# Value tiles ahead of the attention, and three more weight pairs in seven-product form

## The chip, the cores and the metric

The kernel runs on one core of one Trainium2 chip. The core has a matrix engine (TensorE, "PE" in the profile; its weight loads are "PEld"), a vector engine (VectorE, "DVE"), a scalar engine (ScalarE, "ACT"), GpSimd ("POOL") and SyncE ("SP"), which mostly issues transfers. All run beside each other, each in the order of its own queue, and wait for each other by semaphores. The metric is the time of one execution on the device in microseconds; lower is better. Matrix operands lie in the on-chip memory, matrix results in accumulator banks of 128 x 512 fp32, and inputs, outputs and the scratch tensors named `..._d` in DRAM.

## The reference

One layer of a hybrid backbone on two token groups that share the weights: 128 context tokens and 512 latent tokens (an 8 x 64 grid), 1024 channels. Cut to what matters:

```python
h = x * (1 + scale) + shift                       # modulation from c
z = h @ w_in                                      # 1024 -> 4*1024 + 4*1024 + 2*1024
hy, g_h, qkv, g_a, m = split(z)
y_h = (fft_conv(v_h * x1) + u * d) * x0           # Hyena branch, after a 3-tap convolution
q, k, v = qkv                                     # 16 heads of 64
y_a = softmax(q k^T / 8 + bias) v                 # latents: 8 x 16 window and 128 cached keys
p_h = (y_h * silu(g_h)) @ w_bh
p_a = (y_a * silu(g_a)) @ w_ba
out = (sigmoid(m_h) * p_h + sigmoid(m_a) * p_a) @ w_out
x_new = layer_norm(ALPHA * x + gate * out)
```

Returned are the new tokens of both groups and the context group's keys and values. Everything is fp32. The kernel splits an operand into a rounded high half and a low half and takes three passes for a product (high x high, high x low, low x high).

## The kernel before, in words

All 640 tokens are one matrix: `hH` and `hL`, the halves of `h`, hold 8 tiles of 128 channels by 640 tokens and stay on the chip. A weight tile `wall[i]` is 128 x 1024 and gives 128 output channels. A **standard projection** (`proj`, line 168, or line 182 with the low weights last) takes 8 channel tiles x 3 passes x 2 halves of 320 tokens. Its weights come through `wtile`: a load into `raw` (two buffers), a rounded copy `wh` (two buffers) by ScalarE, and a low half `wl` (three buffers), either by VectorE (`split`, lines 101 and 102) or, with `eng="dma"`, as a negated copy by ScalarE to which POOL issues a DMA that adds the raw tile (lines 147 to 149).

A **seven-product pair** (`pair_tile`, line 1146) computes two weight tiles at once. The 2 x 2 blocks (two tiles by two halves of the tokens, with four channel tiles on either side of the sum) are multiplied with seven products of 4 x 3 matmuls. It needs sums of weights (four on VectorE, line 1111, and seven high and low halves), sums of the results (lines 1155 and 1161), and **token sums** t1 to t4 of `hH` and `hL`, made once by `token_sums(r)` for r = 0 and 1 and kept as high and low halves. `prepare` readies a pair's weights; `follow` names the next pair, so that it is prepared while the present one runs.

A **value tile** (`values(m)`, lines 842 to 857) has the tokens as the stationary side and 256 output columns, for four heads: 2 weight tiles, 2 x (48 + 12) matmuls.

The stages: a prologue (modulation), 24 convolution projections with filters and long convolutions beside them, the **hand-over**, the attention, and three projections with the final norm. In the hand-over the main line of work is the last quarter's gated convolution projections, then queries 0, keys 0, values 0, gate 0, queries 1, values 1 and keys 1, with `token_sums(0)` next to the last two. The side line is the last long convolution and `attention_setup`, which gives up the convolution's memory and opens the pools of the attention (`sp`, `at`, `tp`). `weave(main, side, n_main, n_side)` takes n_side steps of the side for n_main steps of the main line. Here a planner orders each engine's instructions, from modelled times; `keep_in_program_order` ties one instruction behind the one traced before it on its engine.

The attention is written for eight pairs of heads (`attend(j)`: scores, softmax, transposes, products with the values one head pair later), each woven with a main line from `mains(j)`: for 0 gate 1, queries 2, keys 2 and `token_sums(1)`; for the others seven-product pairs, with values 2 in 3 and values 3 in 5. There TensorE follows the order of the program (`manual_schedule`); the other engines are planned. Values of head pairs 2m and 2m + 1 come from value tile m, which has a slot of its own (`slot`).

Of the kernel before, what the change touches and what calls it, by code (L numbers as in the profile page):

```python
# [18 lines left out]
NK = 8  # L19
# [26 lines left out]
def tile_hyena_natten_step(ctx: ExitStack, tc: tile.TileContext, a, o):  # L46
# [3 lines left out]
    def f(ap):  # L50
        return ap.bitcast(F32)
# [13 lines left out]
        if pinned[0]:  # L65
            tc.keep_in_program_order(ins)

    def weave(main, side, n_main, n_side):
        done, taken = 0, 0
        for _ in main:  # L70
            done += 1
            while taken * n_main < done * n_side:
                if next(side, StopIteration) is StopIteration:
                    break
                taken += 1
        for _ in side:
            pass
# [34 lines left out]
    def load_pack(i):  # L112
        pack = const.tile([P, sum(n for _, n in PACKS[i])], F32, tag=f"pack{i}", name=f"pack{i}")
        load_to(pack[:], a[f"pack{i}"])
        c0 = 0
        for name, n in PACKS[i]:
            out[name] = pack[:, c0 : c0 + n]
            c0 += n

    load_pack(0)  # L120
    cc, sel = out["cc"], out["sel"]
# [614 lines left out]
    def chain(*gens):  # L736
        for g in gens:
            yield from g

    with tc.manual_schedule(engines={mybir.EngineType.PE, mybir.EngineType.DVE, mybir.EngineType.Activation}):  # L740
        prologue()
    tc.keep_in_program_order(last[0])
# [77 lines left out]

    def keys(j):
        cached_keys(j)
        for hf, p in enumerate((yield from proj(T_K + j, low_last=True))):
            k_half(j, hf, p[:, :HALF])
        yield

    def values(m):
        w = [wtile(T_V + 2 * m + i, width=256) for i in range(2)]
        ps = [acc(f"v{m}_{i}") for i in range(2)]
        v = slot(m, "v", f"v{m}")  # L830
        out[f"v{m}"] = v

        def passes(k):
            wh, wl = w[k // 4][0][k % 4], w[k // 4][1][k % 4]
            return ((hH, wh, k == 0, False), (hL, wh, False, False), (hH, wl, False, k == NK - 1))

        for half in range(2):
            ks = range(4 * half, 4 * half + 4)
            for k in ks:
                for x, wk, first, last in passes(k):  # L840
                    for t in range(4):
                        nc.tensor.matmul(  # L842
                            ps[t // 2][:, t % 2 * 256 : t % 2 * 256 + 256], x[:, k, P * t : P * t + P], wk,
                            start=first and t % 2 == 0, stop=last, skip_group_check=True,
                        )
                yield
            if half:
                for i in range(2):
                    nc.scalar.activation(v[:, 512 * i : 512 * i + 512], ps[i][:], AF.Copy)
# [6 lines left out]
        nc.scalar.activation(v[:, 1024:], pe[:, :256], AF.Copy)  # L856
        nc.sync.dma_start(o["new_v"][:, m * 256 : m * 256 + 256], v[:, :256])
        yield

    N_VALUES = 11  # L860

    def hand_over():
        yield from quarter_tail(3)
        hwa_stack.close()
        out["slots_l"] = left.enter_context(tc.tile_pool(name="slots_l", bufs=1))
        out["slots_q"] = left.enter_context(tc.tile_pool(name="slots_q", bufs=1))
        yield from chain(queries(0), keys(0), values(0), gate_a(0), queries(1))
        out["slots_r"] = left.enter_context(tc.tile_pool(name="slots_r", bufs=1))
        yield from alongside(chain(values(1), keys(1)), token_sums(0), 2)

    tail = ctx.enter_context(ExitStack())
    ac = ctx.enter_context(ExitStack())
    edges, biases = {}, {}

    def attention_setup():
# [3 lines left out]
        tp = left.enter_context(tc.tile_pool(name="tp", bufs=1))  # L879
        at = ac.enter_context(tc.tile_pool(name="at", bufs=1, side="right"))  # L880
        biases[0] = [bias_tile(h) for h in range(2)]
        for b, c in ((0, 0), (3, 320)):
            for h in range(2):
                edges[b, h] = at.tile([P, 384], F32, tag=f"edge{b}{h}", name=f"edge{b}{h}")
                nc.gpsimd.memset(edges[b, h][:, c : c + 64], 0.0)
        yield

    at = sp = tp = None

    def bias_tile(hd):  # L890
        tm = at.tile([P, 1024], F32, tag="tm", bufs=4, name=f"tm{hd}")
# [15 lines left out]
    def probs(j, b, s, tm):  # L907
        lo, hi = TWIN[b]
        res = []
        for h in range(2):  # L910
# [3 lines left out]
            ins = nc.vector.tensor_tensor_reduce(  # L914
                pv, s[h][:, : hi - lo], tm[h][:, lo:hi], -1.0, 3.0e38, ALU.add, ALU.min, accum_out=sm[:, 0:1]
            )
            if j < 2 and h == 0:
                tc.keep_in_program_order(ins)
            nc.scalar.activation(pv, pv, AF.Exp, scale=-1.0, bias=sm[:, 0:1], accum_out=sm[:, 1:2])
            nc.vector.reciprocal(sm[:, 2:3], sm[:, 1:2])  # L920
# [113 lines left out]
                yield  # L1034

    N_ATT = 4

    def gate_a(j):
        out[f"sg{j}"] = sg = at.tile([P, NT], F32, tag="sg", bufs=2, name=f"sg{j}") if j else row(yhp, "yh", "sg0")
        yield from gate_tile(T_GA + j, sg[:], low_last=True)  # L1040
        yield


    SUMS = ("t1", "t3", "t2", "t4")
    tok = {t: [[], []] for t in SUMS}

    def token_sums(r):
        def part(t, i, j):
            return f(t[:, 4 * i + 2 * r : 4 * i + 2 * r + 2, CS[j]])

        def step(dst, i, j, sign):
            for t in (hH, hL):
                nc.vector.tensor_tensor(dst, dst, part(t, i, j), op=ALU.add if sign > 0 else ALU.subtract)

        t1, t2 = (two(row(sp, "s", f"ts{r}{i}", bufs=2)[:]) for i in range(2))

        def keep(name, t):
            pools = [(yhp, "yh", NK + 1)] * 8 if r == 0 else [(tp, "tr", 4)] * 4 + [(sp, "tr", 3)] * 3 + [(at, "tr", 1)]
            for i in range(2):
                pool, tag, bufs = pools[2 * SUMS.index(name) + i]  # L1060
                tok[name][i].append(row(pool, tag, f"{name}_{r}{i}", F32R, bufs))
            split(two(tok[name][0][r][:]), two(tok[name][1][r][:]), t)

        tc.keep_in_program_order(nc.vector.tensor_tensor(t1, part(hH, 0, 1), part(hL, 0, 1), op=ALU.add))
        yield
        nc.vector.tensor_tensor(t2, t1, part(hH, 0, 0), op=ALU.subtract)
        nc.vector.tensor_tensor(t2, t2, part(hL, 0, 0), op=ALU.subtract)
        yield
        keep("t1", t2)
        yield  # L1070
        nc.vector.tensor_tensor(t1, part(hH, 1, 1), t1, op=ALU.subtract)
        nc.vector.tensor_tensor(t1, t1, part(hL, 1, 1), op=ALU.add)
        yield
        keep("t3", t1)
        yield
        step(t2, 1, 1, -1)
        yield
        keep("t2", t2)
        yield
        step(t2, 1, 0, 1)  # L1080
        yield
        keep("t4", t2)

    def operand(name):
        if name in tok:
# [111 lines left out]
    def qk_(j):  # L1197
        return T_Q + j, T_K + j
# [4 lines left out]
    def mix_(m):  # L1203
# [1 line left out]
        return t, t + 1  # L1205

    runs = (
        (mix_(0), qk_(3), mix_(1), qk_(4), ga_(2)), (mix_(2), qk_(5), mix_(3), ga_(4), qk_(6)),
        (mix_(4), qk_(7), mix_(5), ga_(6), mix_(6), mix_(7)),
    )  # L1210
    follow = {x: y for run in runs for x, y in zip(run, run[1:])}

    def alongside(main, side, every, first=0):
        for i, _ in enumerate(main):
            if i >= first and i % every == 0:
                next(side, None)
            yield
        for _ in side:
            pass
# [369 lines left out]
```

## Time and profile before

| | |
|---|---|
| median of 3 runs | 882.67 us (882.23 to 883.29) |
| the profiled execution | 883.84 us |
| its span, first to last instruction | 882.1 us |
| TensorE busy | 868.4 us, 6482 matmuls |
| VectorE busy | 638.4 us |
| ScalarE busy | 432.1 us |
| POOL busy | 129.2 us |
| DMA traffic | 129.21 MB |
| mean granted TensorE clock | 0.994 |

Busy time is the union of an engine's instructions. Matmuls overlap in the array, and their ends are modelled, so TensorE's pace is read from the starts of consecutive matmuls and not from their durations. The chain of work that ended last is followed back from the last instruction, at each step to what released it or to the instruction before it on its engine. In rows of groups of instructions stand the line, engine, operation, output <- inputs, shape and count, then the busy time, the mean of one in ns, and the engine's idle time before them with what ended it. Rows of one line or tile give the least, median and greatest duration in ns and the first and last start in us.

### The profile page before, as it was taken

What the parts mean: (1) busy time and instruction counts of PE and PEld (TensorE: products, weight loads), DVE (VectorE), ACT (ScalarE), POOL (GpSimd) and SP (SyncE); (2) the same over time, 40 slices, a digit from 0 to 9 for tenths busy, and PEclk for the clock granted to TensorE, in tenths of its full rate; (3) what the DMA queues carried; (4) which work ended last, traced back from release to release, by engine and by line L of the source; (5) the groups of instructions that cost most, each with busy time, mean ns of one, the idle gap of its engine ahead of it and who ended that gap; (6) DMA issues with size and microseconds to landing.
All of it is one profiled execution on the core that took longest, in us unless ns stands there. A gap on an engine that the chain in (4) does not pass through costs nothing.

```text
span 882.1 us, 16747 instructions
## 1 busy us (share of the span) xinstructions
PE 868.4 (98%) x6482; PEld 840.5 (95%) x6482; DVE 638.4 (72%) x1276; ACT 432.1 (49%) x926; POOL 129.2 (15%) x133
## 2 busy tenths in 40 slices
PE   8999999999999999999999999999999999999996
PEld 6899999999999999999999999999999999999885
DVE  4686687769559867699887667865788567676666
ACT  3485555645553433366665465655666632243200
POOL 0211010101000000035323222222222200000000
PEclk9999999999999999999999999999999999999999
DMA  9977666566566221262525143433262488446611
GB/s 308 379 193 164 133 134 129 135 142 144 122 145 135 75 93 55 73 216 84 165 75 174 55 151 101 141 106 122 81 191 72 134 307 282 159 151 200 214 59 61
DMA packets 55140, 129.21 MB, mean 146 GB/s; under 512 B 8304, under 2 KB 24436, under 8 KB 55061
## 3 DMA queue, kind: packets, MB, share of 16 engines
q1 hardware_dynamic: 45412, 107.76, 37.5%
q0 software_dynamic: 4032, 14.68, 10.3%
q10 hardware_dynamic: 5616, 5.70, 1.9%
q8 instruction: 51, 0.84, 0.4%
q14 instruction: 29, 0.23, 0.1%
HBM read 113.96 MB, written 14.16 MB: 145 GB/s over the span
## 4 chain that ended last, share of the span: by engine, by line
PE 92%; DVE 4%; DMA 2%; issue 1%; ACT 1%; SPq 0%; DVEq 0%; ACTq 0%
PE mm L168 38%; PE sp L1146 22%; PE out L1413 6%; PE v L842 5%; PE mm L182 3%; PE pt L939 2%; PE s L946 2%; PE s L899 2%; DMA ada<-wada 2%; PE ve L854 1%; PE adaT L251 1%; PE yb L157 1%; PE yb L158 1%; PE yb L156 1%; PE fl L455 1%
## 5 line engine op out<-in xcount | busy, mean ns | idle before, releaser
L1146 PE MATMUL sp<-t,wb 128*128 128x320 f32 x768 | 121.0, 311 | 0.8 <-DVE wb L102 0.8
L1146 PEld LDWEIGHTS sp<-t,wb 128*128 128x128 f32 x768 | 113.9, 188 | 1.6 <-DVE wb L102 1.1
L168 PE MATMUL mm<-hH,wh 128*128 128x320 f32 x480 | 113.8, 314 | 0.3 <-ACT hH L368 0.3
L168 PE MATMUL mm<-hL,wh 128*128 128x320 f32 x480 | 113.3, 312 | 0.0
L168 PE MATMUL mm<-hH,wl 128*128 128x320 f32 x480 | 113.1, 311 | 0.0
L1146 PE MATMUL sp<-hH,wb 128*128 128x320 f32 x384 | 93.2, 313 | 0.0
L168 PEld LDWEIGHTS mm<-hH,wh 128*128 128x128 f32 x480 | 80.6, 189 | 2.6 <-issue 1.4
L168 PEld LDWEIGHTS mm<-hL,wh 128*128 128x128 f32 x480 | 81.2, 189 | 0.9 <-DVE hL L376 0.4
L168 PEld LDWEIGHTS mm<-hH,wl 128*128 128x128 f32 x480 | 81.3, 189 | 0.5
L1146 PEld LDWEIGHTS sp<-hH,wb 128*128 128x128 f32 x384 | 66.0, 188 | 1.9 <-issue 1.9
L101 ACT ACTIVATE wh<-raw 128x1024 fp32r<-128x1024 f32 x31 | 32.9, 1060 | 63.9 <-PE mm L168 35.1
L921 POOL TENSOR_SCALAR p<-p,sm 128x384 f32<-128x384 f32 x32 | 44.9, 1413 | 110.1 <-DVE sm L920 96.2
L149 ACT ACTIVATE wh<-raw 128x1024 fp32r<-128x1024 f32 x28 | 29.8, 1063 | 62.0 <-PE mm L168 62.0
L1146 PE MATMUL sp<-hL,wb 128*128 128x320 f32 x192 | 59.3, 309 | 0.0
L148 POOL DMA_DIRECT2D wl<-wall x28 | 24.3, 869 | 220.9 <-ACT wl L147 160.2
L102 DVE TENSOR_TENSOR wb<-s,wb 128x512 fp32r<-128x512 f32 x64 | 44.6, 711 | 15.7 <-ACT wb L101 15.5
L101 ACT ACTIVATE wb<-s 128x512 fp32r<-128x512 f32 x64 | 39.2, 630 | 25.0 <-DVE s L1111 18.5
L101 ACT ACTIVATE wb<-raw 128x512 fp32r<-128x512 f32 x48 | 30.1, 628 | 35.1 <-PE sp L1146 20.6
L1413 PE MATMUL out<-woh,yhs 128*128 128x512 f32 (+1 forms) x176 | 45.5, 372 | 0.0
L921 POOL TENSOR_SCALAR edge<-edge,sm 128x320 f32<-128x320 f32 x32 | 44.3, 1396 | 2.2 <-DVE sm L920 2.1
L102 DVE TENSOR_TENSOR wl<-raw,wh 128x1024 fp32r<-128x1024 f32 x31 | 37.9, 1221 | 7.7 <-ACT wh L101 7.5
L168 PE MATMUL mm<-yhs,wh 128*128 128x320 f32 x224 | 42.0, 309 | 0.0
(365 smaller groups left out, 2162.2 us busy)
## 6 DMA issues: line engine op xcount, KB each, us to landing
raw<-wall SPq DMA_DIRECT2D x93, 512.0 KB, 3.6
wl<-wall POOLq DMA_DIRECT2D x28, 512.0 KB, 5.7
ada<-wada SPq DMA_DIRECT2D x16, 512.0 KB, 5.9
tm<-bias SPq DMA_DIRECT2D x16, 512.0 KB, 4.5
gate<-wgate SPq DMA_DIRECT2D x8, 512.0 KB, 4.1
wo<-wall SPq DMA_DIRECT2D x8, 512.0 KB, 4.2
xt<-xT SPq DMA_DIRECT2D x8, 320.0 KB, 7.4
dec<-decay SPq DMA_DIRECT2D x20, 128.0 KB, 3.1
```

Source lines behind the costliest of these rows:

```text
L101: hi = nc.scalar.activation(dst_h, src, AF.Copy)
L102: return hi, (eng or nc.vector).tensor_tensor(dst_l, src, f(dst_h), op=ALU.subtract)
L148: nc.gpsimd.dma_start(wl, a["wall"][i], accum_op=ALU.add)
L149: nc.scalar.activation(wh, raw[:], AF.Copy)
L168: nc.tensor.matmul(ps[hf][:, :HALF], wt[k], x[:, hf * HALF : (hf + 1) * HALF], start=(i == 0 and k == 0), stop=(i == lead[2] and k == NK - ...
L182: nc.tensor.matmul(p[:, :HALF], w[i // 2][k], (hH, hL)[i % 2][:, k, cs], start=n == 0, stop=n == len(steps) - 1, skip_group_check=True,)
L842: nc.tensor.matmul(ps[t // 2][:, t % 2 * 256 : t % 2 * 256 + 256], x[:, k, P * t : P * t + P], wk, start=first and t % 2 == 0, stop=last, ...
L899: nc.tensor.matmul(dst[h], x[rows(h), qs], y[rows(h), ks], start=i == 0, stop=i == 2, skip_group_check=True)
L921: nc.gpsimd.tensor_scalar_mul(pv, pv, sm[:, 2:3])
L939: nc.tensor.transpose(pt[:, i * P : i * P + P], x, ident)
L1146: nc.tensor.matmul(dst, wk, x(xi, k), start=j < 4 and k == 0 and i == 0, stop=k == 3 and i == 2, skip_group_check=True,)
L1413: ins = nc.tensor.matmul(dst, m[k][:, c0 : c0 + P], w[:, c : c + n], start=(first and k == 0), stop=(last and k == 5), skip_group_check=True,)
```

## The change

All four value tiles are computed in the hand-over, in the order 1, 2, 3, then queries 0, keys 0, values 0. Values 1, 2 and 3 are evicted into the slots that keys 0 takes later (`k`, `kl`), stored to a DRAM tensor `v_d`, and loaded into their own slots ahead of head pairs 0, 3 and 5 (`values_back`). The low halves of the weights for these tiles, for queries 0 and for keys 0 are made by the POOL-issued DMA (`eng="dma"`). Queries 1 and keys 1, queries 2 and keys 2, and gates 0 and 1 become seven-product pairs in the stages of head pairs 0 and 1; the following pairs with `mix` move accordingly, and all pairs form one chain of `follow`.

The token sums are made earlier: for r = 0 t1, t3, t2 and for r = 1 t1, t3 in `early_sums`, beside the value tiles, with scratch from the convolution's `u` buffers; t2, t4 for r = 1 and t4 for r = 0 in `late_sums`, after `attention_setup`, which waits for `early_sums` to have been written out. Where an operand of a later sum was given up, `again` adds its two halves. `weave` gets a parameter `late`, which holds the side back by one step of the main line in the stages of head pairs 2, 4 and 6. One reduction of head pair 0 is no longer tied to the program order.

```diff
-    def weave(main, side, n_main, n_side):
+    def weave(main, side, n_main, n_side, late=0):
...
-            while taken * n_main < done * n_side:
+            while taken * n_main < (done - late) * n_side:
...
+    def first_sums(r, out_):
+        t2, t1 = (scratch(True, f"ts{r}{i}") for i in range(2))
+        tc.keep_in_program_order(nc.vector.tensor_tensor(t1, part(hH, r, 0, 1), part(hL, r, 0, 1), op=ALU.add))
...
+    def early_sums():
+        t = []
+        yield from first_sums(0, t)
+        yield from second_sum(0, t[0])
+        yield from first_sums(1, t)
+        out["early_sums"] = True
+
+    def late_sums():
+        t = again("t1", 1)
+        yield from second_sum(1, t)
+        yield from third_sum(1, t)
+        yield from third_sum(0, again("t2", 0))
...
-        for hf, p in enumerate((yield from proj(T_Q + j, low_last=True))):
+        for hf, p in enumerate((yield from proj(T_Q + j, eng="dma", low_last=True))):
...
-        w = [wtile(T_V + 2 * m + i, width=256) for i in range(2)]
+        w = [wtile(T_V + 2 * m + i, "dma", width=256) for i in range(2)]
...
+        for i in range(3 if m else 0):
+            nc.sync.dma_start(v_d[m][:, 512 * i : min(512 * i + 512, 1280)], v[i])
...
+    def values_back(m):
+        out[f"v{m}"] = slot(m, "v", f"v{m}")
+        load_to(out[f"v{m}"][:], v_d[m])
...
-        yield from chain(queries(0), keys(0), values(0), gate_a(0), queries(1))
-        out["slots_r"] = left.enter_context(tc.tile_pool(name="slots_r", bufs=1))
-        yield from alongside(chain(values(1), keys(1)), token_sums(0), 2)
+        tp = left.enter_context(tc.tile_pool(name="tp", bufs=1))
+        yield from alongside(chain(values(1), values(2), values(3), queries(0), keys(0), values(0)), early_sums(), 1)
...
     def attention_setup():
-        nonlocal at, sp, tp
+        nonlocal at, sp
+        while "early_sums" not in out:
+            yield
         hy.close()
...
-            if j < 2 and h == 0:
+            if 0 < j < 2 and h == 0:
...
-    weave(hand_over(), chain(gated_conv(2), long_conv(3), long_conv_back(3), gated_conv(3), attention_setup()),
-          6 * NK + N_VALUES, 2 * N_GATED + N_CONV + N_BACK + 1)
+    weave(hand_over(), chain(gated_conv(2), long_conv(3), long_conv_back(3), gated_conv(3), attention_setup(), late_sums()),
+          4 * NK + 3 * N_VALUES + 16, 2 * N_GATED + N_CONV + N_BACK + 7)
+    out["slots_r"] = left.enter_context(tc.tile_pool(name="slots_r", bufs=1))
...
-            0: ((alongside(chain(gate_a(1), queries(2), keys(2)), token_sums(1), 2, 5),), 3 * NK),
-            1: ((mix(0), queries_keys(3)), 2 * N_PAIR),
-            2: ((mix(1), queries_keys(4), gates_a(2)), 3 * N_PAIR),
-            3: ((values(2), mix(2)), N_VALUES + N_PAIR),
+            0: ((queries_keys(1), gates_a(0)), 2 * N_PAIR),
+            1: ((queries_keys(2), mix(0)), 2 * N_PAIR),
+            2: ((queries_keys(3), mix(1), gates_a(2)), 3 * N_PAIR),
+            3: ((queries_keys(4), mix(2)), 2 * N_PAIR),
...
-            5: ((queries_keys(6), values(3), mix(4)), N_VALUES + 2 * N_PAIR),
+            5: ((queries_keys(6), mix(4)), 2 * N_PAIR),
...
+        values_back(1)
         for j in range(8):
             main, n_main = mains(j)
-            weave(chain(*main), attend(j), n_main, N_ATT if j < 7 else N_ATT + 3)
+            if j in (3, 5):
+                values_back(j // 2 + 1)
+            weave(chain(*main), attend(j), n_main, N_ATT if j < 7 else N_ATT + 3, 1 if j in (2, 4, 6) else 0)
```

More of the change, by code (lines that the diff above doesn't have):

```diff
@@ L738, in chain, with part, step, scratch @@
             yield from g
+    SUMS = ("t1", "t3", "t2", "t4")
+    tok = {t: [{}, {}] for t in SUMS}
+    def part(t, r, i, j):
+        return f(t[:, 4 * i + 2 * r : 4 * i + 2 * r + 2, CS[j]])
+    def step(dst, r, i, j, op):
+        for t in (hH, hL):
+            nc.vector.tensor_tensor(dst, dst, part(t, r, i, j), op=op)
+    def scratch(early, name):
+        t = hw.tile([P, NG + 1], F32, tag="u", bufs=4, name=name) if early else at.tile([P, 1024], F32, tag="tm", bufs=4, name=name)
+        return two(t[:, :NT])
@@ new lines, in keep, with again @@
+    def keep(name, r, t):
+        pools = [(yhp, "yh", NK + 1)] * 8 if r == 0 else [(tp, "tr", 4)] * 4 + [(sp, "tr", 3)] * 3 + [(at, "tr", 1)]
+        for i in range(2):
+            pool, tag, bufs = pools[2 * SUMS.index(name) + i]
+            tok[name][i][r] = row(pool, tag, f"{name}_{r}{i}", F32R, bufs)
+        split(two(tok[name][0][r][:]), two(tok[name][1][r][:]), t)
+    def again(name, r):
+        t = scratch(False, f"again_{name}{r}")
+        hi, lo = (f(two(tok[name][i][r][:])) for i in range(2))
+        tc.keep_in_program_order(nc.vector.tensor_tensor(t, hi, lo, op=ALU.add))
+        return t
@@ new lines, in second_sum, with third_sum @@
+    def second_sum(r, t):
+        step(t, r, 1, 1, ALU.subtract)
+        yield
+        keep("t2", r, t)
+        yield
+    def third_sum(r, t):
+        step(t, r, 1, 0, ALU.add)
+        yield
+        keep("t4", r, t)
+        yield
+    def early_sums():
[9 more added lines that the diff above has]
+        yield from third_sum(0, again("t2", 0))
@@ L740, in tile_hyena_natten_step, with alongside @@
+    def alongside(main, side, every, first=0):
+        for i, _ in enumerate(main):
+            if i >= first and i % every == 0:
+                next(side, None)
+            yield
+        for _ in side:
+            pass
+    at = sp = tp = None
     with tc.manual_schedule(engines={mybir.EngineType.PE, mybir.EngineType.DVE, mybir.EngineType.Activation}):
@@ L822, in keys @@
         cached_keys(j)
-        for hf, p in enumerate((yield from proj(T_K + j, low_last=True))):
+        for hf, p in enumerate((yield from proj(T_K + j, eng="dma", low_last=True))):
             k_half(j, hf, p[:, :HALF])
@@ L1036, in tile_hyena_natten_step @@
     N_ATT = 4
[L1038 to L1082, printed above, removed]
     def operand(name):
```

43 lines of the change are left out of this document (27 added, 16 removed).

## The prediction

> **What bounds the kernel now.** I read the busy shares first, then the chain of work that ended last.
>
> ```profile
> span 882.1 us, 16747 instructions
> PE 868.4 (98%) x6482; PEld 840.5 (95%) x6482; DVE 638.4 (72%) x1276; ACT 432.1 (49%) x926; POOL 129.2 (15%) x133
> ...
> PE 92%; DVE 4%; DMA 2%; issue 1%; ACT 1%; SPq 0%; DVEq 0%; ACTq 0%
> ```
>
> TensorE is busy 98% of the span and holds 92% of the chain. But a busy matmul engine is not an engine at its pace: mean durations of about 310 ns overlap. The pace comes from runs in the chain that nothing interrupts:
>
> ```profile
> 344.56 14.08 PE mm L182 x96
> 358.64 3.27 PE v L842 x28
> ...
> 422.71 6.15 PE sp L1146 x42
> ```
>
> 14.08 / 96 = 0.1467 us for a 320-column matmul of a standard projection (L182), 6.15 / 42 = 0.1464 us for one of a seven-product pair (L1146), 3.27 / 28 = 0.1168 us for a 256-column one of a value tile. The Trainium skill ("TensorE: Matmul & The Clock Gate", "Wait — 56ns, not 53.3ns?") gives a warm back-to-back gap of N / 2.4 GHz + about 2.5 ns, an estimate of 135.8 ns for 320 columns; by it the sum below would be 4.9 us instead of 5.3 us. The row is 8% longer, and the measurement decides.
>
> Whether TensorE waits for prepared weights shows in the group of pair matmuls, and how near VectorE is to its limit in the stretches between the borders of the stages (my borders: the first L182, first and last scores, first pair, and so on to the last pair):
>
> ```profile
> L1146 PE MATMUL sp<-t,wb 128*128 128x320 f32 x768 | 121.0, 311 | 0.8 <-DVE wb L102 0.8
> ...
> core 0: us, PE busy (x) PEld busy (x) DVE busy (x) ACT busy (x) POOL busy (x), PEclk, DMA share, GB/s
> 303.70:384.30 80.60, 79.67 (x615) 79.31 (x615) 59.24 (x109) 32.65 (x68) 0.41 (x4) 1.00 0.27 81
> 384.30:409.80 25.50, 25.50 (x188) 24.66 (x188) 24.70 (x59) 15.15 (x42) 16.36 (x10) 1.00 0.49 178
> 409.80:444.50 34.70, 33.90 (x278) 32.46 (x278) 29.73 (x81) 23.32 (x66) 10.45 (x10) 1.00 0.41 128
> ...
> 619.60:665.60 46.00, 46.00 (x362) 44.82 (x361) 37.74 (x95) 28.77 (x71) 11.93 (x10) 1.00 0.42 130
> ```
>
> The first row is the hand-over after the last convolution projection, the second the stage of attention head pair 0, then 1 and 6. In head pair 0 VectorE is busy 24.70 of 25.50 us, and TensorE still never waits; in a stage of three pairs (the last row) VectorE is at 82%. So TensorE's matmul count sets the time, and VectorE has 3% to spare in one place.
>
> **The change, part by part.**
>
> *Matmuls removed.* A standard tile takes 8 x 3 x 2 = 48 matmuls, two take 96, a pair takes 7 x 4 x 3 = 84. Queries and keys 1 and 2 and gates 0 and 1 become three pairs: 36 matmuls less, 36 x 0.1467 = 5.3 us, all on the path that sets the end. Value tiles keep their count (2 x (48 + 12) = 120, so 14.0 us each).
>
> *Where the work moves.* Hand-over: two more value tiles (+28.0), three standard tiles fewer (-21.1): +6.9, so TensorE leaves it near 384.3 + 6.9 = 391.2. Head pair 0: -21.1 + 2 x 12.3 = +3.5. Head pair 3: -14.0 + 12.3 = -1.7. Head pair 5: -14.0. Together -5.3, the same sum. Pairs 1, 2, 4, 6, 7 keep their counts. The side parameter of one step in stages 2, 4 and 6 reorders TensorE's own work; I cost it at nothing, since the stage rows show no wait there; between a wait of 0.8 us gone and 0.8 us new (the whole wait of the pair group).
>
> *Low halves of ten weight tiles (eight for values, queries 0, keys 0) by POOL.*
>
> ```profile
> L102 DVE TENSOR_TENSOR wl<-raw,wh 128x1024 fp32r<-128x1024 f32 x11 | 13.4, 1221 | 3.7 <-ACT wh L101 3.6
> ...
> L147 ACT ACTIVATE wl<-raw x28: 1047/1078/1162, 48.8 to 279.8; 128x1024 fp32r<-128x1024 f32 x28
> ...
> L148 POOL DMA_DIRECT2D wl<-wall x28: 853/862/1028, 50.1 to 281.1; - x28
> ...
> raw<-wall SPq DMA_DIRECT2D x93, 512.0 KB, 3.6
> wl<-wall POOLq DMA_DIRECT2D x28, 512.0 KB, 5.7
> ...
> new_v<-v SPq DMA_DIRECT2D x4, 128.0 KB, 4.2
> ```
>
> VectorE loses 10 x 1.22 = 12.2 us, ScalarE gains 10 x 1.08 = 10.8 us (it is busy 32.65 of 80.60 us there), POOL 10 x 0.86. After the raw weights, the chain is 1.08 + 0.86 + 5.7 = 7.6 us; a weight tile of the values lasts 60 x 0.1168 = 7.0 us and there are three low buffers, two of them ahead: 14.0 us of cover. POOL is busy 0.41 us in the hand-over, so nothing is queued behind these issues. Cost taken: 0; the ends are 0 and what rival C says.
>
> *Values 1 to 3 through DRAM.* Three stores each (256, 256, 128 KB) and one 640 KB load each. Nearest row: 128 KB of new_v in 4.2 us. The next writer of the two slots is the next value tile's eviction, some 7 us or more later (half a tile of matmuls), and each load has a whole stage before its first use. The stores stand in SP's queue behind their eviction and ahead of weight loads: at worst one load (3.6 us) is late by one eviction, under the cover above. Cost 0, with up to 1 us for the upper end; a gain is excluded, since nothing is removed.
>
> *Token sums.* 26 VectorE operations become 28 (two recompute a sum from its halves): 17 in the hand-over, 11 after the attention memory opens. The rows of head pair 0's stretch:
>
> ```profile
> L102 DVE TENSOR_TENSOR t<-ts,t 128x640 fp32r<-128x640 f32 x5 | 4.3, 865 | 0.1
> L1053 DVE TENSOR_TENSOR ts<-ts,hL 128x640 f32<-128x640 f32 x4 | 3.3, 813 | 0.0
> L1053 DVE TENSOR_TENSOR ts<-ts,hH 128x640 f32<-128x640 f32 x3 | 2.9, 963 | 0.1
> L102 DVE TENSOR_TENSOR wl<-raw,wh 128x1024 fp32r<-128x1024 f32 x2 | 2.4, 1218 | 0.0
> ...
> L1072 DVE TENSOR_TENSOR ts<-ts,hL 128x640 f32<-128x640 f32 x1 | 1.0, 987 | 0.0
> ...
> L1066 DVE TENSOR_TENSOR ts<-ts,hH 128x640 f32<-128x640 f32 x1 | 0.8, 814 | 0.0
> ...
> L102 DVE TENSOR_TENSOR wb<-raw,wb 128x512 fp32r<-128x512 f32 x1 | 0.7, 679 | 0.0
> L1111 DVE TENSOR_TENSOR s<-raw,raw 128x512 f32<-128x512 f32 x1 | 0.7, 675 | 0.0
> ```
>
> An operation on 640 columns takes some 0.84 us here. Early: 17 x 0.84 = 14.3 us, into a stretch where VectorE has 80.6 - 59.2 = 21.4 us free, plus 9 x 1.22 = 11.0 us of weight halves (the eleven of the row above, which covers 304 to 418, less the two of head pair 0's stretch). Late: 11 x 0.84 = 9.2 us, when the memory opens. Hidden, if it opens in time:
>
> ```profile
> 378.39 0.41 POOL L885 MEMSET edge<- 128x64 f32 x4 [96.39 <-PE y L713]
> ...
> 378.36 0.80 SPq L63 DMA_DIRECT2D tm<-bias  x2
> ...
> 385.25 0.33 PE L899 MATMUL s<-k,q 64*128 64x128 f32 x2
> ...
> 388.04 0.48 DVE L914 CUSTOM_DVE_ANT_0 edge<-s,tm 128x320 f32<-128x320 f32 x1
> ```
>
> It opens at 378.4, right behind the last convolution transposes (y), 6.9 us before the first score. After the change the first score comes near 392, so the cover grows to about 13.5 us. Of that, the second product of the first pair needs sum t2: one recomputation, two steps, one split, some 4 us.
>
> *VectorE in head pair 0.* A pair costs VectorE 7 low halves, 4 weight sums, 5 combinations:
>
> ```profile
> L102 DVE TENSOR_TENSOR wb<-s,wb 128x512 fp32r<-128x512 f32 x48 | 33.4, 708 | 13.9 <-ACT wb L101 13.8
> ...
> L1161 DVE TENSOR_TENSOR c<-sp,u 128x320 f32<-128x320 f32 x36 | 17.5, 486 | 12.2 <-PE sp L1146 12.1
> L1111 DVE TENSOR_TENSOR s<-raw 128x512 f32<-128x512 f32 x12 | 8.5, 710 | 0.1
> ```
>
> 11 x 0.71 + 5 x 0.49 = 10.2 us. The stage gains 20.4 us for two pairs and 1.0 for two more gate halves; it loses the token groups above (4.3 + 3.3 + 2.9 + 1.0, and four such as L1066's of 0.8 each, 14.7 in all), 2.4 of weight halves and 1.4 of the first pair's preparation. Net +2.9 us by durations, so VectorE does about 27.6 us in a stage of 29.0 us: 95%, against 97% now. Cost taken: 0 beyond the wait of 0.8 us that is there already.
>
> *Sum.* -5.3 us. The profiled execution took 883.84 us (span 882.1 and 1.7 around it): 878.5. It stands 1.2 us above the median, so the median becomes 877.4.
>
> **Rivals.**
> *A, VectorE binds in head pair 0.* For it: 97% today, and the margin is only 1.4 us; the late sums and the splits of queries and keys 0 crowd against its front. If the 9.2 us of late sums overran the 12.8 us between opening and 391.2 by 3 to 4 us (an opening at 382 to 386, with 4 us of splits), the end moves by that: 877.4 + 3.7 = 881.1, no measurable change. Against: TensorE ran through 97% without a wait.
> *B, slower: the attention memory opens late and VectorE's queue blocks.* The early sums use the convolution's scratch, which must be free before that memory opens; VectorE works in order, and the late sums wait for the memory with the subtractions of queries and keys 0 possibly behind them. Those free the accumulators that value tile 0 needs, around 391.2 - 14.0 = 377. If all 14.3 us of early sums lengthened the path to the opening (392.7), TensorE would lose up to 15.7 us: 893. It passes 884.4 from 7 us on, an opening past 384. Against: the 21.4 + 11.0 us of room above; the order in the hand-over is planned with these waits in view.
> *C, POOL's halves come late.* From a landing of 14.0 - 1.9 = 12.1 us on, up from 5.7, each of ten tiles stalls by the excess; at 13 us, 9 us more: 886. Against: 28 such loads serve the convolutions today, and their matmuls show no wait:
>
> ```profile
> L168 PE MATMUL mm<-hH,wl 128*128 128x320 f32 x480 | 113.1, 311 | 0.0
> ```
>
> The Trainium skill ("SBUF — State Buffer", "Who interferes with whom") says that copies and one-input operations on VectorE can lock POOL out while it writes descriptors. No issue above took more than 1.03 us, so the trace shows no such lock, and the time would stay as forecast.
>
> **How the numbers follow.** Forecast (874.5 to 880.5) 0.66; A 0.14, a third of it still over 0.2% faster; B 0.13; C 0.04; a new wait elsewhere 0.03. The lower end adds the waits that may go: the hand-over's 80.60 - 79.67 = 0.9, head pair 1's 0.8, and 1.2 for the order of work. The upper end takes in A and the near half of B: 885. A difference under 0.2% (1.8 us) can't be told from none. Faster 0.66 + 0.05 + 0.01, same 0.10, slower 0.18.
>
> **What would show it.** Right: 1,596 pair matmuls at 0.1464 us; the first of them near 393; head pair 5's stage about 34 us instead of 47.7; 16 fewer low halves of whole weight tiles on VectorE (the wl group of L102). Wrong by A: waits of pair matmuls for wb or c over 2 us before 425. By B: edge's memset past 384, and value matmuls waiting for VectorE or ScalarE. By C: value matmuls waiting for a DMA.

## The result: 882.5 to 875.0 us

The changed kernel takes 874.96 us in the median of 4 runs (874.31 to 875.37), against 882.50 us for the kernel before, run beside it (882.23 to 883.29, 4 runs). The ratio is 0.9912 with an interval of 0.9895 to 0.993: 7.5 us less. Two more sets of runs gave 0.9918 (0.9899 to 0.9937) and 0.9914 (0.9894 to 0.9934). The forecast was 877.4 us, in a range of 874.5 to 885.0.

The profiled execution of the changed kernel took 874.77 us, 9.1 us less than that of before. Its page, by the span, the busy shares, the shares of the chain that ended last, and the costliest group:

```profile
span 873.0 us, 16814 instructions
PE 861.0 (99%) x6446; PEld 833.0 (95%) x6446; DVE 645.6 (74%) x1310; ACT 447.1 (51%) x952; POOL 130.0 (15%) x143
PE 95%; DMA 2%; ACT 2%; DVE 1%; issue 0%; POOL 0%; DVEq 0%; ACTq 0%; POOLq 0%
L1189 PE MATMUL sp<-t,wb 128*128 128x320 f32 x912 | 142.0, 310 | 0.0
```

TensorE has 36 matmuls less (6482 to 6446), as the count in the prediction says, and the pair matmuls (now line 1189) have lost their idle time of 0.8 us. The waits of TensorE, as engine, line, what it waited for, total us, times and longest, have four rows of before that matter here:

```profile
PE adaT L251 <- DMA ada<-wada: 2.0, 1, 2.0
PE adaT L268 <- POOL spare L310: 1.6, 1, 1.6
PE c_X L156 <- ACT uh L101: 0.9, 1, 0.9
PE sp L1146 <- DVE wb L102: 0.8, 1, 0.8
```

After the change the first two are still there, and the last two have gone; nothing has come in their place:

```profile
PE adaT L270 <- POOL spare L312: 1.6, 1, 1.6
PE adaT L253 <- DMA ada<-wada: 1.6, 2, 1.1
PE mm L170 <- ACT hH L370: 0.3, 1, 0.3
PE modT L270 <- DVE mod L362: 0.3, 1, 0.3
```

To keep the prologue out of the comparison I measure one **stretch** in every kernel: from the first transpose `ut` of a convolution to the start of the last pair matmul. The rows give first and last start in us. Before:

```profile
L620 PE MATMUL ut<-pack,u x40: 270/284/357, 99.0 to 334.9; 128*128 128x128 f32 x40
...
L1146 PE MATMUL sp<-hH,wb x384: 302/308/417, 409.8 to 704.2; 128*128 128x320 f32 x192
```

After:

```profile
L622 PE MATMUL ut<-pack,u x40: 270/283/291, 97.2 to 332.1; 128*128 128x128 f32 x40
...
L1189 PE MATMUL sp<-hH,wb x456: 302/309/417, 388.4 to 694.9; 128*128 128x320 f32 x152
```

The stretch shrinks from 704.2 - 99.0 = 605.2 us to 694.9 - 97.2 = 597.7 us: -7.5 us, the whole difference of the medians. The other 1.6 us between the two profiled executions lie outside: -1.8 us in the prologue, which the change does not touch, and +0.2 us in the tail (882.1 - 704.2 = 177.9 against 873.0 - 694.9 = 178.1).

The stages of the hand-over, of head pair 0 and of head pair 5, each as from:to, length, then busy time and count of PE, PEld, DVE, ACT, POOL, granted clock, DMA share, GB/s:

```profile
302.40:388.30 85.90, 85.90 (x706) 85.81 (x705) 63.86 (x116) 44.48 (x78) 7.31 (x12) 1.00 0.68 172
388.30:417.40 29.10, 29.10 (x213) 28.26 (x213) 26.31 (x72) 20.18 (x55) 13.41 (x10) 1.00 0.46 154
576.70:610.40 33.70, 33.70 (x279) 32.51 (x278) 27.15 (x78) 21.51 (x58) 10.85 (x10) 1.00 0.37 115
```

TensorE is busy all the time in all three. The stages of head pairs 0 and 5 take 29.1 and 33.7 us (29.0 and 34 were worked out); VectorE does 26.31 of 29.10 us in head pair 0, 90% where 95% was expected. The hand-over ends at 388.3 us instead of the 391.2 that was worked out, and the first pair starts at 388.4 instead of near 393: 1.8 us of that is the prologue, and 1.2 us is the wait at c_X that went (below).

### The profile page after: what moved, and what is told of

It reads as the page before. It is cut to its first block, busy times and chain, and to the rows that moved or that the text cites. A ratio compares the mean times of both kernels' runs of the same rounds, so it can differ in the third digit from the quotient of the medians.

```text
span 873.0 us, 16814 instructions
## 1 busy us (share of the span) xinstructions
PE 861.0 (99%) x6446; PEld 833.0 (95%) x6446; DVE 645.6 (74%) x1310; ACT 447.1 (51%) x952; POOL 130.0 (15%) x143
## 4 chain that ended last, share of the span: by engine, by line
PE 95%; DMA 2%; ACT 2%; DVE 1%; issue 0%; POOL 0%; DVEq 0%; ACTq 0%; POOLq 0%
PE mm L170 36%; PE sp L1189 27%; PE out L1454 6%; PE v L926 5%; PE pt L1028 3%; PE s L1035 3%; PE s L988 2%; PE mm L184 2%; DMA ada<-wada 2%; PE ve L938 1%; DMA wl<-wall 1%; PE adaT L253 1%; PE adaT L270 1%; PE yb L159 1%; PE yb L158 1%; PE yb L160 1%
## 5 line engine op out<-in xcount | busy, mean ns | idle before, releaser
L1189 PE MATMUL sp<-t,wb 128*128 128x320 f32 x912 | 142.0, 310 | 0.0
L1189 PEld LDWEIGHTS sp<-t,wb 128*128 128x128 f32 x912 | 135.2, 188 | 0.9 <-issue 0.7
L1189 PE MATMUL sp<-hH,wb 128*128 128x320 f32 x456 | 111.2, 314 | 0.0
L1189 PEld LDWEIGHTS sp<-hH,wb 128*128 128x128 f32 x456 | 78.5, 188 | 2.3 <-issue 2.1
L151 ACT ACTIVATE wh<-raw 128x1024 fp32r<-128x1024 f32 x38 | 40.4, 1062 | 73.4 <-PE mm L170 65.5
L150 POOL DMA_DIRECT2D wl<-wall x38 | 33.0, 868 | 299.5 <-ACT wl L149 238.8
L1189 PE MATMUL sp<-hL,wb 128*128 128x320 f32 x228 | 70.4, 309 | 0.0
L102 DVE TENSOR_TENSOR wb<-raw,wb 128x512 fp32r<-128x512 f32 x57 | 40.6, 712 | 8.6 <-ACT wb L101 8.6
L1189 PEld LDWEIGHTS sp<-hL,wb 128*128 128x128 f32 x228 | 42.9, 188 | 0.0
L149 ACT ACTIVATE wl<-raw 128x1024 fp32r<-128x1024 f32 x38 | 40.8, 1075 | 0.0
```

The source lines that it names most:

```text
L102: return hi, (eng or nc.vector).tensor_tensor(dst_l, src, f(dst_h), op=ALU.subtract)
L149: nc.scalar.activation(wl, raw[:], AF.Copy, scale=-1.0)
L150: nc.gpsimd.dma_start(wl, a["wall"][i], accum_op=ALU.add)
L151: nc.scalar.activation(wh, raw[:], AF.Copy)
L1189: nc.tensor.matmul(dst, wk, x(xi, k), start=j < 4 and k == 0 and i == 0, stop=k == 3 and i == 2, skip_group_check=True,)
```

## The experiments

The question is which part of the change gave the 7.5 us: the matmul count explains 5.3. And was the margin in the opening of the attention's memory and on VectorE, on which the forecast rested, as large as the prediction said? In the table the ratio is to the kernel before on the same chip, and the stretch is read from the profile of each, as above (605.2 before, 597.7 after).

| kernel | median us (runs) | ratio, interval | stretch us |
|---|---|---|---|
| three pairs as standard tiles | 882.15 (12) | 0.9984, 0.997 to 0.9999 | 602.9 |
| low halves back on VectorE | 874.04 (4) | 0.99, 0.9881 to 0.9919 | 597.3 |
| the same again | 874.7 (4) | 0.9907, 0.9888 to 0.9926 | 597.3 |
| before, with low halves by POOL | 883.35 (12) | 1.0007, 0.9996 to 1.0019 | 605.2 |
| side line not held back | 874.92 (6) | 0.9917, 0.9897 to 0.9937 | 597.9 |
| memory opened in mid value tile 0 | 882.76 (10) | 1.0003, 0.9986 to 1.002 | 603.6 |
| memory opened behind value tile 0 | 882.02 (10) | 1.0, 0.9985 to 1.0014 | 605.0 |
| only the order of writing of that | 875.75 (4) | 0.9922, 0.9894 to 0.9949 | 597.7 |
| more work on VectorE in head pair 0 | 878.44 (8) | 0.9952, 0.9938 to 0.9967 | 600.4 |
| after, again | 874.9 (6) | 0.9918, 0.9899 to 0.9937 | 597.7 |
| after, third | 875.15 (5) | 0.9914, 0.9894 to 0.9934 | 597.7 |

**Three pairs as standard tiles.** Everything of the change is kept but the seven products: queries, keys 1 and 2 and gates 0 and 1 are six standard tiles in the same stages.

```diff
-            qk_(1), ga_(0), qk_(2), mix_(0), qk_(3), mix_(1), ga_(2), qk_(4), mix_(2), qk_(5), mix_(3), ga_(4),
+            mix_(0), qk_(3), mix_(1), ga_(2), qk_(4), mix_(2), qk_(5), mix_(3), ga_(4),
...
-            0: ((queries_keys(1), gates_a(0)), 2 * N_PAIR),
-            1: ((queries_keys(2), mix(0)), 2 * N_PAIR),
+            0: ((plain(1), gate_a(0), gate_a(1)), 4 * NK),
+            1: ((plain(2), mix(0)), 2 * NK + N_PAIR),
```

> The changed kernel with its three new pairs taken back: queries and keys 1 and 2 and gates 0 and 1 are six standard tiles again, in the stages of head pairs 0 and 1; the value tiles, token sums and POOL's low halves stay where the change put them. Theory (the matmul count gives 5.3 us, the rearrangement around it the other 2): 875.0 + 36 x 0.1467 = 880.3 us, between 879.6 and 881.2, and no wait of TensorE for VectorE in the profile. Rival (the gain comes mostly from the rearrangement, which unloads VectorE): below 878. Rival (the pairs are worth more than their count, because standard tiles meet waits here): above 881.5, with these waits in the profile.

The median, 882.15 us, is above what was expected, and it mixes two groups: five of the twelve runs took 879.7 to 880.0 us, with a mean granted clock of 0.997 or 0.998, and the others 882.1 to 884.0 with 0.994 to 0.996 (the last section tells of that clock; where these runs lost it, no trace shows). By the medians alone the three pairs would be worth 7.2 us; the stretch, which leaves the prologue out, is what separates the parts here. The profiled execution is of the first group, which lies where 880.3 us was expected. Its stretch:

```profile
L622 PE MATMUL ut<-pack,u x40: 270/283/291, 96.9 to 331.7; 128*128 128x128 f32 x40
...
L1189 PE MATMUL sp<-hH,wb x384: 302/309/417, 442.2 to 699.8; 128*128 128x320 f32 x192
```

699.8 - 96.9 = 602.9 us. From here to the changed kernel it is -5.2 us, and the 36 matmuls at 0.1467 us are 5.3. From the kernel before to here it is -2.3 us, with the same matmul count. The two waits, c_X and sp, are gone in this kernel too. What they cost is read from the starts on TensorE (start, length, instruction, count, and in brackets the idle time with its releaser):

```profile
323.79 0.60 PE L713 MATMUL y<-pack,E 128*128 128x128 f32 x4
324.22 0.72 PE L620 MATMUL ut<-pack,u 128*128 128x128 f32 x4
325.88 0.39 PE L156 MATMUL c_X<-uh,dftH 128*128 128x256 f32 x1 [0.93 <-ACT uh L101]
...
414.82 3.83 PE L1146 MATMUL sp<-t,wb 128*128 128x320 f32 x25
419.45 0.85 PE L1146 MATMUL sp<-t,wb 128*128 128x320 f32 x4 [0.80 <-DVE wb L102]
```

25 matmuls at 0.1464 us from 414.82 end their turn at 418.48; the next starts at 419.45, 1.0 us late. Four transposes take 324.22 - 323.79 = 0.43 us; those from 324.22 end their turn at 324.65; c_X starts 1.2 us late. A wait listed as 0.8 or 0.9 us thus costs 1.0 or 1.2, and the two 2.2 us: the 2.3 us of the stretch.

After the change the same four transposes and c_X stand further apart on TensorE:

```profile
321.89 0.65 PE L622 MATMUL ut<-pack,u 128*128 128x128 f32 x4
...
324.94 0.28 PE L158 MATMUL c_X<-uh,dftH 128*128 128x256 f32 x1
```

3.05 us lie between their starts instead of 1.66, filled with value matmuls: ScalarE's copy has time to finish. So the first wait went by a change of order beside it. Why the weights of the first pair are ready in time now, no run takes alone.

**Low halves back on VectorE, and the same again.**

```diff
-        w = [wtile(T_V + 2 * m + i, "dma", width=256) for i in range(2)]
+        w = [wtile(T_V + 2 * m + i, width=256) for i in range(2)]
```

and so for queries 0 and keys 0.

> The changed kernel with the low halves of the ten weight tiles (values, queries 0, keys 0) made by VectorE again instead of by ScalarE and POOL's DMA. VectorE gets 12.2 us more work between 302 and 388 us, where it is busy 63.9 of 85.9. Theory (these halves are hidden on either engine): 875.0, between 874.5 and 876. Rival (taking them off VectorE is what removed the two waits of 0.9 and 0.8 us): 876.5 to 877.5, with a wait of TensorE for ScalarE or VectorE near 325 us or near the first pairs. Rival (the convolution's end and with it the attention memory move later and the margin is used up): above 878.

> The changed kernel with all ten low halves on VectorE once more, beside the changed kernel. In the traces the stretch from the convolutions to the last pair was 645.6 us against 646.3. If that is real: 0.5 to 1.0 us below the changed kernel of this call. If it is chance: within 0.3 us of it.

In both traces the stretch is 0.3 us shorter (597.34 against 597.67), and no wait of TensorE comes back. The second median, 874.7 us, is 0.45 us below the changed kernel beside it (875.15), between the two outcomes that had been named, so a cost of POOL's halves of that size is not excluded. The ten low halves by POOL gain nothing in this kernel, and neither did they remove the two waits.

**The kernel before, with low halves by POOL** for its own queries 0 and keys 0 and values 0 and 1.

```diff
-        w = [wtile(T_V + 2 * m + i, width=256) for i in range(2)]
+        w = [wtile(T_V + 2 * m + i, "dma" if m < 2 else None, width=256) for i in range(2)]
```

> The kernel before, with POOL's DMA for the low halves of the six weight tiles of queries 0, keys 0 and values 0 and 1 in its hand-over, and nothing else. Theory (the low halves are hidden, the two waits come from the order of the convolution's last steps and of the first pair): 882.5, between 881.8 and 883.2. Rival (VectorE's load in the hand-over makes the waits): 880.8, and the profile without the wait of 0.9 us for the first spectrum matmuls.

No gain: 883.35 us. The wait at c_X went here too, but the one in the first pair grew:

```profile
411.62 3.68 PE L1146 MATMUL sp<-t,wb 128*128 128x320 f32 x24
415.82 0.56 PE L1146 MATMUL sp<-t,wb 128*128 128x320 f32 x2 [0.52 <-ACT wb L101]
417.78 1.74 PE L1146 MATMUL sp<-t,wb 128*128 128x320 f32 x10 [1.40 <-DVE wb L102]
```

24 matmuls from 411.62 end at 415.13 and two from 415.82 at 416.11: 0.7 + 1.7 us of gaps, where before had 1.0. What is won in the hand-over, TensorE waits for at the first pair, which came earlier than its weights. The changed kernel differs there: its first pairs are prepared without such a wait.

**Side line not held back.**

```diff
-            weave(chain(*main), attend(j), n_main, N_ATT if j < 7 else N_ATT + 3, 1 if j in (2, 4, 6) else 0)
+            weave(chain(*main), attend(j), n_main, N_ATT if j < 7 else N_ATT + 3, 0)
```

> The changed kernel without holding the attention back by one step in head pairs 2, 4 and 6 (late = 0 everywhere). Theory (it reorders TensorE's own work, and no wait depends on it): 875.0, between 874.4 and 875.6. Rival (without it, attention products wait for the softmax at the start of the three-pair stages): 876 to 878, with waits of TensorE in those three stages.

874.92 us, and 0.2 us in the stretch: the parameter is worth nothing that can be told.

**The attention's memory opened later.** An additional transpose, whose result is not used, is tied on TensorE behind the first half of value tile 0, and the release of the convolution's memory behind it.

```diff
+            if half == 0 and m == 0:
+                out["hold"] = True
...
-        while "early_sums" not in out:
+        while "early_sums" not in out or "hold" not in out:
             yield
+        held = aux("held")
+        tc.keep_in_program_order(nc.tensor.transpose(held[:, :P], out["E3"][:, 0, :P], out["ident"]))
         hy.close()
```

> The changed kernel with one more transpose of the convolution's E tile (result unused), tied on TensorE behind the first half of value tile 0, so that the convolution's memory is given up, and the attention's opened, near 381 us instead of 376.2. Theory (cover: nothing needs this memory before the second product of the first pair near 391, some 4 us of sums after the opening): no change, 875.0, between 874.3 and 875.8; memset of edge near 381; no wait of TensorE. Rival B of the prediction (VectorE's queue blocks behind the late sums, and value tile 0 waits for its accumulators): each us of later opening costs one, 5 us, 879 to 881, with the wait in the value matmuls.

My expectation fell: 882.76 us, by the median the whole gain. The trace is of the fastest of the ten runs (880.55 us, clock 0.997; the others 0.989 to 0.996) and shows 6.0 us of loss in the stretch (603.64 against 597.67); what the slower ones lost beyond that is in no trace. The memory's opening shows in the memset of `edge` on POOL, the end of the late sums in the low halves of `t` on VectorE (least, median and greatest ns, first and last start). The first fence is the changed kernel, the second this one:

```profile
L976 POOL MEMSET edge<- x4: 151/151/153, 376.2 to 376.4; 128x64 f32 x4
...
L102 DVE TENSOR_TENSOR t<-again_t,t x3: 806/811/814, 385.8 to 390.7; 128x640 fp32r<-128x640 f32 x3
```

```profile
L980 POOL MEMSET edge<- x4: 151/152/152, 382.9 to 383.1; 128x64 f32 x4
...
L102 DVE TENSOR_TENSOR t<-again_t,t x3: 807/814/824, 388.5 to 403.7; 128x640 fp32r<-128x640 f32 x3
```

The memory opens 6.7 us later. The last of the late sums, the low half of t4 for r = 0 (the last start), ends at 391.5 us in the changed kernel, 15.3 us behind the opening; here it ends at 404.5, 21.6 us behind it. TensorE, in the first pair:

```profile
399.93 0.30 PE L1193 MATMUL sp<-hH,wb 128*128 128x320 f32 x1
402.40 0.41 PE L1193 MATMUL sp<-t,wb 128*128 128x320 f32 x1 [2.17 <-ACT t L101]
404.53 1.80 PE L1193 MATMUL sp<-t,wb 128*128 128x320 f32 x7 [1.72 <-DVE t L102]
```

The matmuls that wait are those of the product with t4. They start at 402.40 - 399.93 - 0.15 = 2.3 us late, and the second again 404.53 - 402.40 - 0.15 = 2.0. The rest of the 6.0 us is the clock, which falls to half right behind these waits (columns as above; the clock is the third number from the end):

```profile
400.00:404.00 4.00, 0.64 (x3) 0.19 (x1) 4.00 (x16) 3.89 (x14) 4.00 (x4) 1.00 0.24 57
404.00:408.00 4.00, 3.47 (x15) 3.47 (x16) 3.30 (x8) 1.12 (x2) 4.00 (x3) 0.64 0.89 353
408.00:412.00 4.00, 4.00 (x30) 4.00 (x30) 4.00 (x10) 1.91 (x7) 1.70 (x2) 0.94 0.06 16
```

0.36 x 4 + 0.06 x 4 = 1.7 us of full-speed time lost. 2.3 + 2.0 + 1.7 = 6.0, the loss in the stretch.

**Memory opened behind value tile 0.** The same, with `hold` set behind the tile's last matmul.

> The same with the transpose tied behind the last matmul of value tile 0: the memory opens near 388.5 us, 12 us later than in the changed kernel. Theory (cover): the second product of the first pair is due near 391.7 and its sum t2 comes 4 to 10 us after the opening, 392.5 to 398; the pair's preparation and the late sums crowd VectorE afterwards. So a loss of 1 to 7 us, 876 to 882, as waits of pair matmuls for VectorE, none in the value matmuls. Rival B: 12 us, 887, most of it ahead of the end of value tile 0. Rival (the margin is wider than I think): 875.

The opening comes at 388.8 us, and the time, 882.02 us, is in the range expected, but by another chain than rival B's: no value matmul waits. Now the first late sum, t2, is late:

```profile
L980 POOL MEMSET edge<- x4: 151/152/152, 388.8 to 389.1; 128x64 f32 x4
...
392.01 1.04 PE L1193 MATMUL sp<-t,wb 128*128 128x320 f32 x6
394.98 0.41 PE L1193 MATMUL sp<-t,wb 128*128 128x320 f32 x1 [1.93 <-ACT t L101]
396.91 7.25 PE L1193 MATMUL sp<-t,wb 128*128 128x320 f32 x29 [1.52 <-DVE t L102]
```

392.01 + 6 x 0.1464 = 392.89, so 2.1 us late, and then 1.8. The clock behind it:

```profile
392.00:396.00 4.00, 1.46 (x9) 0.97 (x7) 4.00 (x14) 3.35 (x12) 1.19 (x2) 1.00 0.99 391
396.00:400.00 4.00, 3.09 (x11) 3.09 (x12) 3.93 (x11) 2.46 (x7) 2.98 (x3) 0.52 0.59 181
400.00:404.00 4.00, 4.00 (x19) 3.90 (x18) 3.86 (x6) 0.00 (x0) 3.01 (x2) 0.63 0.43 134
```

0.48 x 4 + 0.37 x 4 = 3.4 us more; 2.1 + 1.8 + 3.4 = 7.3, which is the stretch's loss again.

**Only the order of writing.** To hold the memory back, the late sums had also to be written later in the program. This kernel keeps that and drops the transpose.

```diff
-        held = aux("held")
-        tc.keep_in_program_order(nc.tensor.transpose(held[:, :P], out["E3"][:, 0, :P], out["ident"]))
```

> The kernel with the opening near 381 us (e5) without its extra transpose: the late sums are written out as late as there, after the first half of value tile 0, and nothing holds the convolution's memory back. In e5 the memory opened 6.7 us later (382.9) and the stretch from the convolutions to the last pair took 5.9 us more; TensorE waited 2.3 and 2.0 us for token sum t4 and then ran at half clock for 3.4 us, which costs another 1.7. Theory (the later opening pushes the late sums into head pair 0's softmax): the memory opens near 376 again, no wait of pair matmuls, 875 us. Rival (the order in which VectorE is given the late sums does it, since the planner takes work in the order written): the waits for t4 and the half clock stay, 879 to 882.

The stretch is that of the changed kernel (597.7 us), with no wait of a pair matmul. All its times stand 3.3 us later by its prologue; so corrected, the opening is unmoved, but the last late sum is not:

```profile
L978 POOL MEMSET edge<- x4: 152/152/153, 379.4 to 379.7; 128x64 f32 x4
...
L102 DVE TENSOR_TENSOR t<-again_t,t x3: 810/818/824, 386.8 to 399.0; 128x640 fp32r<-128x640 f32 x3
```

399.0 - 3.3 against 390.7 is 5.0 us later, from the order of writing alone, and it costs nothing. With the later opening it is 403.7, 8.0 us more, and that is past the start of the product, which in the changed kernel is at 400.2 us:

```profile
400.23 1.92 PE L1189 MATMUL sp<-t,wb 128*128 128x320 f32 x12
```

So the later opening made the loss, on top of an order that had used up 5.0 of the 8.7 us between 391.5 and 400.2.

**More work on VectorE in head pair 0.** Fourteen additional additions of 320 columns into an unused tile, some 6.6 us, beside the main line of head pair 0.

```diff
+    def load(n):
+        d = at.tile([P, HALF], F32, tag="d", name="d")
+        for i in range(n):
...
+            tc.keep_in_program_order(nc.vector.tensor_tensor(d[:], x, f(hL[:, i % 8, :HALF]), op=ALU.add))
...
-            0: ((queries_keys(1), gates_a(0)), 2 * N_PAIR),
+            0: ((alongside(chain(queries_keys(1), gates_a(0)), load(14), 1),), 2 * N_PAIR),
```

> The changed kernel with 14 additions of 128 x 320 on VectorE (results unused), spread over the stage of head pair 0, each tied behind what was traced before it: 14 x 0.47 = 6.6 us more in a stretch where VectorE is busy 26.3 of 29.1 us. Theory (VectorE is the next bound there, as rival A of the prediction has it, with 2.8 us of room and weights that are ready 2.7 us or more before use): 6.6 - 2.8 = 3.8 us over, of which the lead of the weights takes up to 2.7: 875.5 to 879, with waits of pair matmuls for VectorE in that stage. Rival (VectorE's order bends around it, and its slack in the next stage takes the load): 875.0, no wait.

878.44 us; the stretch grows by 2.7. The stage of head pair 0 in this kernel, from the start of its first pair to that of the third (it begins 1.8 us later by its prologue: the first `ut` is at 99.0 instead of 97.2), and the waits of TensorE:

```profile
390.10:421.90 31.80, 29.89 (x213) 28.27 (x212) 31.20 (x85) 19.47 (x54) 13.75 (x10) 1.00 0.41 141
```

```profile
PE sp L1189 <- DVE wb L102: 1.4, 2, 1.2
PE sp L1189 <- ACT wb L101: 0.5, 1, 0.5
```

The stage takes 31.8 us instead of 29.1, the 2.7 us of the stretch. VectorE is busy 31.20 us of it, 98%, and TensorE waits for weights: VectorE is the next bound in this stage, as rival A has it, and 6.6 - 2.7 = 3.9 us is an estimate of the work that it could take first (the trace has the additions at 7.1 us in all, which would make it 4.4). The additions are also tied into VectorE's order, so this run does not separate the load from the fixed order.

**After, again and third.** The changed kernel without an edit, beside the other sets.

> The changed kernel itself once more, on the chip of the other runs: 875.0, between 874.3 and 876.

> The changed kernel itself, for the comparison with e2: 874.9, between 874.3 and 876.

The medians agree within 0.25 us, and the stretch is 597.7 us all three times.

## Why the prediction was right or wrong

The direction and the main term were right; the forecast was 2.4 us too high, by a term that was sized at nothing. The 874.96 us measured lie 0.5 us above the lower end of the range, which these waits had been used to set.

- **Matmuls removed, -5.3 us: right.** The stretch differs by 5.2 us between six standard tiles and three pairs. The pace held, and TensorE has no gap that takes it back.
- **The term that was mis-sized: the waits that go.** The prediction named the hand-over's 0.9 us and the pair's 0.8, and put them into the lower end alone. They went, and each was worth its whole gap by the starts, 1.2 and 1.0 us: 2.3 us in the stretch between the kernel before and the one with standard tiles. 5.3 + 2.3 is the -7.5 us measured, within the rounding of the rows. The waits stood in rows that were read, and the change rebuilt the work around both; an expected value of half of them would have been nearer than none. That this was not sure is shown by the kernel before with POOL's halves, where the wait moved on instead.
- **Low halves by POOL at 0: right within 0.3 us.** Taken away, they make the stretch 0.3 us shorter. Rival C has no support: none of TensorE's matmul waits above is for such a transfer.
- **Side line held back at 0: right** (0.2 us in the stretch).
- **Values through DRAM at 0 to +1:** no run takes this alone. The accounts above leave nothing for it, and no wait of TensorE in the changed kernel names these loads.
- **Token sums hidden: right here, with a wrong reason.** The prediction took t2 as the one that must be ready, some 4 us behind the opening. In the changed kernel the first of the three low halves that `late_sums` makes ends at 385.8 + 0.8 = 386.6, 10.4 us behind the opening, and with the memory opened at 388.8 us TensorE was released by it at 396.9, 8.1 us behind. And t2 is not the first to run out: t4, the last of the chain, falls into head pair 0's own work on VectorE and bound TensorE when the memory opened at 382.9. The cover of 13 us, real as it is (376.2 to a first score at 389.3), holds with less to spare than was worked out.
- **Rival A** puts 3.7 us on an opening at 382 to 386 us. Its mechanism, late sums that overrun, is what the later opening showed; the price is 6.0 us in the stretch, since the clock adds 1.7. Its other half, VectorE at its limit, begins some 3.9 us of work further on (the estimate above).
- **Rival B** lets value tile 0 starve behind VectorE's queue, at a loss from an opening past 384 us on. With the opening at 382.9 or 388.8 no value matmul waited; the loss came at the pair. But these kernels do not put its mechanism to the test, since they also write the late sums later, and at 388.8 value tile 0 had ended. In the changed kernel VectorE does the last subtraction that frees an accumulator for keys 0 (`kl<-mm`, L894) at 375.6 us, ahead of the first late sum at 378.8, so that the late sums have none of them behind them. A late opening is about as dear as the rival said: 6.0 and 7.3 us in the stretch.

## What to carry to other kernels

Where an engine runs at its pace nearly all the time, pace times count gives a change's main term to a tenth of a microsecond; then go through the few waits listed for that engine, measure each by the starts on both sides of it, and give those whose surroundings the change rebuilds a share in the forecast, not only in the range. Price a moved chain by its last member and by what else its engine does by then, not by its first user. A wait of TensorE of some 2 us can cost 1.7 or 3.4 us more in the clock behind it.

## What was not expected of the hardware

TensorE's granted clock can fall to half behind short waits. The kernel before shows it in its profiled prologue, where it waits 2.0 us for the transfer of `ada`:

```profile
18.00:24.00 6.00, 5.70 (x34) 5.29 (x35) 4.21 (x10) 2.50 (x6) 0.24 (x1) 0.52 1.03 398
24.00:30.00 6.00, 6.00 (x79) 5.33 (x82) 2.43 (x6) 2.45 (x5) 1.75 (x2) 0.91 1.03 415
```

(0.48 + 0.09) x 6 = 3.4 us are lost, so the clock was at half for 6.8 us. The changed kernel, whose longest wait for `ada` was 1.1 us, ending at 27.9 us, lost nothing around it:

```profile
24.00:30.00 6.00, 4.43 (x55) 3.73 (x54) 2.26 (x5) 2.74 (x5) 0.00 (x0) 1.00 1.02 412
```

It is part of why the two profiled executions differ by more than the medians. The prologues of two more kernels show the same: the one with only the order of writing behind a wait of 1.8 us for `ada`, with one of 0.5 us shortly before it,

```profile
28.00:32.00 4.00, 3.73 (x29) 3.53 (x30) 0.52 (x3) 0.74 (x2) 0.00 (x0) 0.62 1.04 421
32.00:36.00 4.00, 4.00 (x14) 3.37 (x14) 1.27 (x2) 1.89 (x4) 2.56 (x2) 0.53 1.02 409
```

(0.38 + 0.47) x 4 = 3.4 us lost, and the one with more work on VectorE behind 2.1 us (a clock of 0.98 from 24 to 28 us and 0.59 from 28 to 32: 1.7 us lost). With the two kernels with a later opening, whose waits were 2.2 + 1.7 and 1.9 + 1.5 us, the half clock lasted 3.4 or 6.8 us in all five. It did not follow the 0.5 + 1.4 us of the kernel before with POOL's halves, nor the weight waits of the kernel with more work on VectorE (0.5 and 1.2 at most), whose stage row above has a clock of 1.00. Nor did it follow 1.3 + 0.8 us for `ada` in the third set of the changed kernel, so the total waited does not decide alone: those 2.1 us passed, the single 2.0 us of before did not. The Trainium skill ("TensorE: Matmul & The Clock Gate", "What's actually happening") tells of a free-running window of 3413 ns and of half speed "after ≥1 idle window (~3.4µs)". The lengths agree, one window or two; that a whole idle window is needed does not agree with the 2.0 us wait here, and the measurement decides. What share of a window must be idle, these runs leave open.
